# Conditioning columns from small fp32 products in a transformer layer

## The chip, the cores and the metric

The kernel runs on one core of a Trainium2 chip. The metric is the time of one execution on the device, in microseconds. The engines of the core are TensorE (PE, matrix products; PEld is its loading of the stationary operand), VectorE (DVE), ScalarE (ACT), GpSimd (POOL) and SyncE (SP), whose queue issues most DMA transfers.

## The reference, cut to what matters

One layer: two gated feed-forward networks with a token mixer between them (attention heads and mLSTM heads), on 256 tokens of width 2048, all in fp32. Each of the three parts is conditioned by a shift, a scale and a gate, nine vectors of 2048 that come from one row `c`:

```python
ada = (jax.nn.silu(c) @ w_ada + b_ada)[:, None, :]
sh1, sc1, g1, sh2, sc2, g2, sh3, sc3, g3 = jnp.split(ada, N_ADA, axis=-1)
h = _swiglu(_modulate(x, sh1, sc1), ffn1_w_in, ffn1_w_out)
x = _layernorm(ALPHA * x + 0.5 * (1 + g1) * h, ln1_g, ln1_b)
h = _token_mixer(_modulate(x, sh2, sc2), ...)
...
```

`_modulate(x, shift, scale)` is `_layernorm(x) * (1 + scale) + shift`. `w_ada` has 2048 rows of 18432 columns, 151 MB.

## The kernel before, in words

The feed-forward networks and the mixer run on TensorE. Weights arrive as fp32, ACT rounds them to fp32r (`hi`, L142), DVE forms the rest (`lo`, L143), and three products (L369 to L371) replace one of fp32. The tokens are columns (256 moving columns) in most stages and rows (512 moving columns) in the output projections. The stages in the profile's names: `s` and `gu_f` the input side of the first network, `o_f` its output projection, `mo`, `pr_f`, `pr_m`, `b_fv` the mixer's inputs, `o_mx` its output projection, `ge`, `fh`, `gf`, `fs` and `gu_f` the second network.

The nine conditioning vectors are summed beside this work. For 1024 columns at a time, 16 row tiles `ar` of 128 x 1024 are loaded (512 KB each, two buffers), and DVE multiplies each with its column of silu(c) and adds it to `acc` (L155, L157), so that `acc` holds 128 partial sums per column, one in each partition. What is left is the sum over the partitions.

- `first_ada0` and `first_ada` make shift and scale of the first part at the start; `first_columns` (L716) sums with eight products per 1024 columns that have `acc` as stationary operand and a column of ones as moving operand.
- `ada_pair(v, js)` makes shift and scale of the other two parts, v = 3 and v = 6. A set, one `j`, is 512 columns of the shift and the same 512 of the scale. The result is wanted as columns, features over the partitions, in `scsh`. For each half `i`, `ada_split` splits 512 columns into `ahi` (ACT) and `alo` (DVE); two pauses later `ada_sum` (L170) sums with two products that have the ones as stationary operand. That leaves the sums as a row, the same in each partition, in `bc`; a multiplication with the identity (`dg`, L188) and a reduction (L190) pick each feature's own partition, and a last add brings in the bias (L192).
- `ada_gate` makes the three gates, which are wanted as rows, with the same `ada_split` and `ada_sum`.

The sets and gates form one queue of generators, `ada_queue`. The big stages call `pump(n)` at fixed places: it takes `n` steps of the queue, a step being one row tile, and stops for this call at a pause (`PAUSE`); what it was owed stays owed. `need(n)` empties the queue up to the n-th part before a place that needs it, without regard to pauses. `pinned` puts what a step issues on an engine behind the newest split of weights on that engine. The order on each engine is otherwise made by a list scheduler from the order in the program and from buffers that come free. At the two boundaries between the parts the order of DVE and ACT is written out by hand.

The small buffers of the pool `ap` are shared by tag: `ahi` and `alo` of 2 KB per partition, `acc` of 4 KB, `araw` twice 4 KB. `tri`, `crow` and `brow` are used at the start only, in the places of the tags `ahi` and `alo`.

Of the kernel before, what the change touches and what calls it, by code (L numbers as in the profile page):

```python
# [7 lines left out]
F32 = mybir.dt.float32  # L8
F32R = mybir.dt.float32r
AF = mybir.ActivationFunctionType  # L10
ALU = mybir.AluOpType
AX = mybir.AxisListType
PSUM = bass.MemoryType.PSUM

P = 128
T = 256
D = 2048
KD = D // P
# [14 lines left out]
def layer_kernel(  # L33
# [8 lines left out]
    V, S, G_, PE, SP = nc.vector, nc.scalar, nc.gpsimd, nc.tensor, nc.sync  # L42
# [16 lines left out]
    ap = ctx.enter_context(tc.tile_pool(name="ap", bufs=1))  # L59
# [7 lines left out]
    def aux_tile(name):  # L67
        return pa.tile([P, 512], F32, tag="aux", name=name)


    ident = cst.tile([P, P], F32, name="ident")
    G_.memset(ident, 0.0)
    G_.affine_select(out=ident, in_=ident, compare_op=ALU.not_equal, fill=1.0, base=0,
                     pattern=[[-1, P]], channel_multiplier=1)
    tri = ap.tile([P, 2 * P], F32, tag="ahi", name="tri")
    G_.memset(tri, 1.0)
    G_.affine_select(out=tri[:, :P], in_=tri[:, :P], compare_op=ALU.is_ge, fill=0.0, base=0,
                     pattern=[[1, P]], channel_multiplier=-1)
# [3 lines left out]
    ones, onesr = triu1[:, P:], trir[:, P:]  # L82


    crow = ap.tile([KD, P], F32, tag="alo", name="crow")
    SP.dma_start(crow, c[0].rearrange("(k p) -> k p", p=P))
    res = cst.tile([P, 2, D], F32, name="res")
    for a in range(2):
# [7 lines left out]
    bcol = cst.tile([P, 9, KD], F32, name="bcol")  # L96
# [2 lines left out]
    G_.memset(mhalf, -0.5)  # L99

    def load_bcol():
        brow = ap.tile([72, 2, P], F32, tag="ahi", name="brow")
        SP.dma_start(brow, b_ada[0].rearrange("(h r p) -> r h p", h=2, p=P))
        bps = aux_tile("bps")
        for i in range(2):
            PE.transpose(bps[:, i * 72:(i + 1) * 72], brow[:, i, :], ident[:72, :72])
        V.tensor_copy(bcol.rearrange("p v k -> p (v k)"), bps[:, :144])
        for v in (1, 4, 7):
            V.tensor_scalar_add(bcol[:, v, :], bcol[:, v, :], 1.0)
# [31 lines left out]
    def split(src, hi, lo):  # L141
        S.copy(hi, src)  # L142
        return V.tensor_tensor(out=lo, in0=src, in1=hi.bitcast(F32), op=ALU.subtract)  # L143


    scsh = cst.tile([P, 9, KD], F32, name="scsh")
# [3 lines left out]
    def pair_cols(v, j):  # L150
        return w_ada[0, :, v * D:(v + 2) * D].rearrange("k (v n) -> k v n", v=2)[:, :, j * 512:(j + 1) * 512]

    def ada_acc(acc, raw, k):
        if k == 0:
            V.tensor_scalar_mul(acc, raw, csil[:, k:k + 1])  # L155
        else:
            V.scalar_tensor_tensor(out=acc, in0=raw, scalar=csil[:, k:k + 1], in1=acc,  # L157
                                   op0=ALU.mult, op1=ALU.add)


    def ada_split(acc, tag):
        ahi = ap.tile([P, 512], F32R, tag="ahi", name=f"ahi{tag}")
        alo = ap.tile([P, 512], F32R, tag="alo", name=f"alo{tag}")
        split(acc, ahi, alo)
        return ahi, alo

    def ada_sum(parts, tag):
        bc = aux_tile(f"bc{tag}")
        for i in range(2):
            PE.matmul(bc, onesr, parts[i], start=i == 0, stop=i == 1)  # L170
        return bc

    def ada_pair(v, js):
        for j in js:
            src = pair_cols(v, j)
            acc = ap.tile([P, 2, 512], F32, tag="acc", name=f"acc{v}_{j}")
            for k in range(KD):
                raw = ap.tile([P, 2, 512], F32, tag="araw", bufs=2, name=f"ar{v}_{j}_{k}")
                SP.dma_start(raw, src[k * P:(k + 1) * P])
                ada_acc(acc, raw, k)  # L180
                yield
            for i in range(2):
                parts = ada_split(acc[:, i, :], f"{v}_{j}_{i}")
                for _ in range(2):
                    yield PAUSE
                bc = ada_sum(parts, f"{v}_{j}_{i}")
                dg = ap.tile([P, 4, P], F32, tag="alo", name=f"dg{v}_{j}_{i}")
                V.tensor_tensor(out=dg, in0=bc.rearrange("p (a b) -> p a b", b=P),  # L188
                                in1=ident.unsqueeze(1).to_broadcast([P, 4, P]), op=ALU.mult)
                V.tensor_reduce(out=scsh[:, v + i, j * 4:(j + 1) * 4], in_=dg, axis=AX.X, op=ALU.add)  # L190
            cs = scsh[:, v:v + 2, j * 4:(j + 1) * 4]
            V.tensor_tensor(out=cs, in0=cs, in1=bcol[:, v:v + 2, j * 4:(j + 1) * 4], op=ALU.add)  # L192

    def ada_gate(v, s):
        for j in range(2):
            c0 = v * D + j * 1024
            acc = ap.tile([P, 1024], F32, tag="acc", name=f"acc{v}_{j}")
            for k in range(KD):
                raw = ap.tile([P, 1024], F32, tag="araw", bufs=2, name=f"ar{v}_{j}_{k}")
                SP.dma_start(raw, w_ada[0, k * P:(k + 1) * P, c0:c0 + 1024])  # L200
                ada_acc(acc, raw, k)
                yield
            for i in range(2):
                parts = ada_split(acc[:, i * 512:(i + 1) * 512], f"{v}_{j}_{i}")
                yield PAUSE
                if i == 0:
                    G_.dma_start(gate[:, j * 1024:(j + 1) * 1024], b_ada[0:1, c0:c0 + 1024].to_broadcast([P, 1024]))
                yield PAUSE
                bc = ada_sum(parts, f"{v}_{j}_{i}")
                gs = gate[:, j * 1024 + i * 512:j * 1024 + (i + 1) * 512]  # L210
                V.scalar_tensor_tensor(out=gs, in0=bc, scalar=1.0, in1=gs, op0=ALU.add, op1=ALU.add)
                if s != 1.0:
                    V.tensor_scalar_mul(gs, gs, s)

    ada_left = {}
    PAUSE = 1
# [450 lines left out]
    def entry_of(load, got, u0, u1):  # L667
        for u in range(u0, u1):
            got[u] = []
            for item in load(u):  # L670
                got[u].append(item)
                yield
# [181 lines left out]
    for k in range(KD):  # L854
        next(fa)
        if k == 4:
            load_bcol()
    with tc.manual_schedule(engines={mybir.EngineType.DVE, mybir.EngineType.Activation}):
        next(fa)
    ada_queue(ada_gate(2, 0.5), ada_pair(3, range(4)), ada_pair(6, range(2)), ada_gate(5, 1.0),  # L860
              ada_pair(6, range(2, 3)), ada_pair(6, range(3, 4)), ada_gate(8, 0.5))
    for j in range(4):
        fa = first_ada(j + 1) if j < 3 else load_mixer_smalls()
# [73 lines left out]
    fence, _, xs, ws = boundary(*ent["f"], lgb, 3, "1", xT, entry_of(mo_load, mow, 3, 6), KD, raws)  # L937
# [459 lines left out]
    for j in range(2, 10):  # L1397
# [6 lines left out]
        for f in range(2):  # L1404
            i = 2 * j + f
# [10 lines left out]
    for j in range(2, 10):  # L1416
# [7 lines left out]
        for f in range(2):  # L1424
            i = 2 * j + f
# [51 lines left out]
```

## Time and profile before

| | |
|---|---|
| times of 3 runs | 1929.67, 1932.37, 1935.84 us; median 1932.37 |
| profiled execution | 1936.38 us, of which span 1934.7 us |
| mean granted clock of TensorE | 0.994 |
| DMA | 510.90 MB, mean 264 GB/s |
| row tiles issued from SP in `w_ada` | 227 of 512 KB, 5.6 us from issue to landing |
| first and last sum of a pair (L188) | 500.3 and 1308.9 us |

The columns of a row of groups are: line, engine, operation, output and inputs by the program's names, shapes and count, then the busy time and the mean of one in ns, then the idle time of the engine just before them and what ended it. A row of the timeline has start and length in us; `x4` merges four records, and an idle time before it stands in brackets with what ended it.

### The profile page before, as it was taken

To read this page: it belongs to the slowest core of one execution; us is meant where nothing else is said; L and a number is where in the kernel's file an instruction comes from. 1 tells how busy PE (TensorE), PEld (TensorE's weight loads), DVE (VectorE), ACT (ScalarE), POOL (GpSimd) and SP (SyncE) were. 2 spreads that over 40 slices of the span, in tenths; PEclk is the share of its full clock that TensorE was granted. 3 is DMA by queue.
4 is the path that set the end of the run, shared out by engine and by line. 5 is a ranking of instruction groups with operands and counts; after the bars stand their busy time and mean duration, and the time that the engine had idled before them with its cause. 6 is when DMAs were issued, how large, how long until landed. Compare 5 with 4: busy or idle time off the path is not lost.

```text
span 1934.7 us, 32285 instructions
## 1 busy us (share of the span) xinstructions
PE 1895.6 (98%) x13085; PEld 1722.5 (89%) x13085; DVE 1485.6 (77%) x1838; ACT 954.6 (49%) x1352; POOL 56.3 (3%) x82
## 2 busy tenths in 40 slices
PE   6999999999999999999999999999999999999997
PEld 3999999999988888698998786999999999988886
DVE  5779989777889898888888789777766665555776
ACT  3554454443454555845755545555444444444552
POOL 1111100000000000100000000000000000000000
PEclk8999999999999999999999999999999999999999
DMA  9978969899998786498888884997776776655552
GB/s 352 372 260 317 324 222 318 296 309 312 304 337 311 264 302 222 155 325 297 274 293 285 278 289 173 300 307 247 253 252 227 261 238 196 238 185 188 194 196 87
DMA packets 295709, 510.90 MB, mean 264 GB/s; under 512 B 10850, under 2 KB 158722, under 8 KB 294536
## 3 DMA queue, kind: packets, MB, share of 16 engines
q1 hardware_dynamic: 287784, 480.53, 73.3%
q0 software_dynamic: 7776, 28.32, 4.2%
q8 instruction: 102, 1.67, 0.3%
q14 instruction: 47, 0.39, 0.1%
HBM read 506.71 MB, written 2.10 MB: 263 GB/s over the span
## 4 chain that ended last, share of the span: by engine, by line
PE 78%; issue 11%; DMA 6%; DVE 3%; ACT 1%; POOL 0%; SPq 0%; DVEq 0%; ACTq 0%; POOLq 0%
PE gu_f L369 8%; PE gu_f L371 8%; PE gu_f L370 8%; PE o_f L369 8%; PE o_f L371 8%; PE o_f L370 8%; PE s L369 4%; PE s L371 4%; PE s L370 4%; DMA ar<-in_w_ada_dram 3%; PE fh L369 2%; PE fh L371 2%; PE fh L370 2%; PE fs L369 1%; PE fs L370 1%
## 5 line engine op out<-in xcount | busy, mean ns | idle before, releaser
L157 DVE SCALAR_TENSOR_TENSOR acc<-ar,csil,acc 128x1024 f32<-128x1024 f32 x242 | 308.0, 1274 | 84.4 <-DMA ar<-in_w_ada_dram 82.8
L369 PE MATMUL s<-xhi_f,hi_s 128*128 128x256 f32 x768 | 213.2, 278 | 1.1 <-ACT hT1a L825 1.1
L370 PE MATMUL s<-xlo_f,hi_s 128*128 128x256 f32 x768 | 213.1, 277 | 0.0
L371 PE MATMUL s<-xhi_f,lo_s 128*128 128x256 f32 x768 | 212.8, 277 | 0.0
L371 PE MATMUL gu_f<-xhi_f,lo_f2i 128*128 128x256 f32 x768 | 212.0, 276 | 0.0
L369 PE MATMUL gu_f<-xhi_f,hi_f2i 128*128 128x256 f32 x768 | 212.0, 276 | 0.0
L370 PE MATMUL gu_f<-xlo_f,hi_f2i 128*128 128x256 f32 x768 | 212.0, 276 | 0.0
L143 DVE TENSOR_TENSOR lo_f2i<-raw_f2i,hi_f2i 128x1024 fp32r<-128x1024 f32 x96 | 117.5, 1224 | 88.3 <-ACT hi_f2i L142 88.2
L371 PE MATMUL gu_f<-xhi_f,lo_f1i 128*128 128x256 f32 x640 | 176.7, 276 | 0.0
L369 PE MATMUL gu_f<-xhi_f,hi_f1i 128*128 128x256 f32 x640 | 176.7, 276 | 0.0
L370 PE MATMUL gu_f<-xlo_f,hi_f1i 128*128 128x256 f32 x640 | 176.7, 276 | 0.0
L142 ACT CAST hi_f2i<-raw_f2i 128x1024 fp32r<-128x1024 f32 x96 | 100.8, 1050 | 135.1 <-PE gu_f L370 124.3
L142 ACT CAST hi_s<-raw_s 128x1024 fp32r<-128x1024 f32 x96 | 100.3, 1052 | 130.1 <-PE s L370 83.7
L369 PEld LDWEIGHTS s<-xhi_f,hi_s 128*128 128x128 f32 x768 | 144.7, 189 | 1.3 <-ACT hT1a L825 1.3
L370 PEld LDWEIGHTS s<-xlo_f,hi_s 128*128 128x128 f32 x768 | 144.9, 189 | 0.2 <-DVE xlo_f L300 0.2
L371 PEld LDWEIGHTS s<-xhi_f,lo_s 128*128 128x128 f32 x768 | 144.9, 189 | 0.0
L370 PEld LDWEIGHTS gu_f<-xlo_f,hi_f2i 128*128 128x128 f32 x768 | 144.1, 188 | 0.2
L369 PEld LDWEIGHTS gu_f<-xhi_f,hi_f2i 128*128 128x128 f32 x768 | 144.1, 188 | 0.2
L371 PEld LDWEIGHTS gu_f<-xhi_f,lo_f2i 128*128 128x128 f32 x768 | 144.1, 188 | 0.0
L143 DVE TENSOR_TENSOR lo_f2o<-raw_f2o,hi_f2o 128x1024 fp32r<-128x1024 f32 x88 | 107.8, 1225 | 44.9 <-ACT hi_f2o L142 44.8
L143 DVE TENSOR_TENSOR lo_s<-raw_s,hi_s 128x1024 fp32r<-128x1024 f32 x96 | 115.8, 1223 | 29.0 <-ACT hi_s L142 29.0
L369 PE MATMUL o_f<-hi_f2o,hh 128*128 128x512 f32 x344 | 135.2, 393 | 0.0
(502 smaller groups left out, 5383.9 us busy)
## 6 DMA issues: line engine op xcount, KB each, us to landing
ar<-in_w_ada_dram SPq DMA_DIRECT2D x227, 512.0 KB, 5.6
raw_f2i<-in_ffn_w_in_dram SPq DMA_DIRECT2D x48, 1024.0 KB, 5.2
raw_s<-in_ffn_w_in_dram SPq DMA_DIRECT2D x47, 1024.0 KB, 7.4
raw_f1o<-in_ffn_w_out_dram SPq DMA_DIRECT2D x44, 1024.0 KB, 6.7
raw_f2o<-in_ffn_w_out_dram SPq DMA_DIRECT2D x44, 1024.0 KB, 5.0
raw_f1i<-in_ffn_w_in_dram SPq DMA_DIRECT2D x40, 1024.0 KB, 7.8
ar<-in_w_ada_dram POOLq DMA_DIRECT2D x48, 512.0 KB, 6.9
raw_mxo<-in_w_out_dram SPq DMA_DIRECT2D x16, 1024.0 KB, 6.3
```

The lines of the kernel that those rows point to most:

```text
L142: S.copy(hi, src)
L143: return V.tensor_tensor(out=lo, in0=src, in1=hi.bitcast(F32), op=ALU.subtract)
L157: V.scalar_tensor_tensor(out=acc, in0=raw, scalar=csil[:, k:k + 1], in1=acc, op0=ALU.mult, op1=ALU.add)
L369: PE.matmul(o, ah, bh, start=start, stop=False)
L370: PE.matmul(o, ah, bl, start=False, stop=False)
L371: PE.matmul(o, al, bh, start=False, stop=stop)
```

## The change

A set of `ada_pair` is no longer split. ACT copies the 1024 sums of `acc` as they are into `rows`; four pauses in a row follow, where there were two in each half; then eight fp32 products, each with 128 columns of `rows` as stationary operand and one column of ones as moving operand, put the sums into `cp` (a PSUM tile `cc`) as columns, and one DVE add brings in the bias and writes `scsh`. The two tags `ahi` and `alo` become one tag `as` of 4 KB, which `ada_split` of the gates uses as one tile with two parts; `tri` and `brow` move to `as`, `crow` to `acc`.

```diff
-    tri = ap.tile([P, 2 * P], F32, tag="ahi", name="tri")
+    tri = ap.tile([P, 2 * P], F32, tag="as", name="tri")
...
-    crow = ap.tile([KD, P], F32, tag="alo", name="crow")
+    crow = ap.tile([KD, P], F32, tag="acc", name="crow")
...
-        brow = ap.tile([72, 2, P], F32, tag="ahi", name="brow")
+        brow = ap.tile([72, 2, P], F32, tag="as", name="brow")
...
     def ada_split(acc, tag):
-        ahi = ap.tile([P, 512], F32R, tag="ahi", name=f"ahi{tag}")
-        alo = ap.tile([P, 512], F32R, tag="alo", name=f"alo{tag}")
-        split(acc, ahi, alo)
-        return ahi, alo
+        parts = ap.tile([P, 2, 512], F32R, tag="as", name=f"as{tag}")
+        split(acc, parts[:, 0, :], parts[:, 1, :])
+        return parts[:, 0, :], parts[:, 1, :]
...
                 yield
+            rows = ap.tile([P, 2, 512], F32, tag="as", name=f"rows{v}_{j}")
+            S.copy(rows, acc)
+            for _ in range(4):
+                yield PAUSE
+            cp = aux_tile(f"cc{v}_{j}")[:, :8].rearrange("p (v k) -> p v k", v=2)
             for i in range(2):
-                parts = ada_split(acc[:, i, :], f"{v}_{j}_{i}")
-                for _ in range(2):
-                    yield PAUSE
-                bc = ada_sum(parts, f"{v}_{j}_{i}")
-                dg = ap.tile([P, 4, P], F32, tag="alo", name=f"dg{v}_{j}_{i}")
-                V.tensor_tensor(out=dg, in0=bc.rearrange("p (a b) -> p a b", b=P),
-                                in1=ident.unsqueeze(1).to_broadcast([P, 4, P]), op=ALU.mult)
-                V.tensor_reduce(out=scsh[:, v + i, j * 4:(j + 1) * 4], in_=dg, axis=AX.X, op=ALU.add)
-            cs = scsh[:, v:v + 2, j * 4:(j + 1) * 4]
-            V.tensor_tensor(out=cs, in0=cs, in1=bcol[:, v:v + 2, j * 4:(j + 1) * 4], op=ALU.add)
+                for q in range(4):
+                    PE.matmul(cp[:, i, q:q + 1], rows[:, i, q * P:(q + 1) * P], ones[:, 0:1], start=True, stop=True)
+            V.tensor_tensor(out=scsh[:, v:v + 2, j * 4:(j + 1) * 4], in0=cp, in1=bcol[:, v:v + 2, j * 4:(j + 1) * 4],
+                            op=ALU.add)
```

## The prediction

> **What bounds the kernel now.** I read the page first, for the engines and for the chain that ended last.
>
> ```profile
> span 1934.7 us, 32285 instructions
> PE 1895.6 (98%) x13085; PEld 1722.5 (89%) x13085; DVE 1485.6 (77%) x1838; ACT 954.6 (49%) x1352; POOL 56.3 (3%) x82
> PE 78%; issue 11%; DMA 6%; DVE 3%; ACT 1%; POOL 0%; SPq 0%; DVEq 0%; ACTq 0%; POOLq 0%
> ```
>
> TensorE (PE) is busy for 98% of the span, VectorE (DVE) for 77%, and the chain runs through PE for 78%. Matmuls are pipelined, so a busy PE need not be a full one. The second view is therefore the table of stretches, to see where PE really stands still.
>
> ```profile
> 40.00:1640.00 1600.00, 1587.93 (x11611) 1476.05 (x11610) 1274.02 (x1589) 808.90 (x1174) 48.16 (x66) 1.00 0.82 277
> 820.00:1005.00 185.00, 183.09 (x1376) 174.32 (x1376) 156.38 (x245) 105.53 (x185) 0.00 (x0) 0.99 0.90 302
> 1005.00:1165.00 160.00, 154.08 (x898) 133.53 (x897) 126.33 (x166) 79.16 (x139) 2.24 (x2) 1.00 0.84 281
> 1165.00:1215.00 50.00, 48.10 (x179) 31.44 (x179) 44.19 (x89) 30.06 (x58) 4.72 (x5) 1.00 0.52 179
> ```
>
> The columns after the length are the busy times of PE, PEld (its weight loads), DVE, ACT and POOL, then clock, DMA share and GB/s. Between 40 and 1640 us PE is idle for 1600.00 - 1587.93 = 12.07 us. Of these 1.91 lie in 820 to 1005 us, 5.92 in 1005 to 1165 us and 1.90 in 1165 to 1215 us: the token mixer and the boundary behind it hold 9.7 of the 12.07. Elsewhere PE has its next operand every time. All eight sets of columns that the change touches are made inside this stretch, as the rows below show. The third view is the list of PE's waits in the same stretch.
>
> ```profile
> PE ptp L1093 <- ACT s L1088: 2.5, 2, 1.4
> PE sps L1201 <- DVE dm L1207: 1.9, 1, 1.9
> PE ptp L1093 <- DVE gate L211: 1.6, 1, 1.6
> PE o_mx L370 <- DVE lo_mxo L143: 1.2, 2, 0.7
> PE s L369 <- ACT hT1a L825: 1.1, 1, 1.1
> ```
>
> No wait of PE is put down to `dg`, `scsh` or a row transfer of a pair. What the change takes off DVE is nowhere the thing that PE waits for last, by these rows; what it puts on PE has no idle time to fall into.
>
> **The change part by part: PE.** One set is 2 x 512 columns (`ada_pair`, one `j`). Before, each half costs two matmuls of `onesr` with 512 moving columns. The timeline of one half:
>
> ```profile
> 499.21 0.28 PE L371 MATMUL gu_f<-xhi_f,lo_f1i 128*128 128x256 f32 x1
> 499.55 0.28 PE L371 MATMUL gu_f<-xhi_f,lo_f1i 128*128 128x256 f32 x1
> 499.68 0.39 PE L170 MATMUL bc<-ahi,trir 128*128 128x512 f32 x1
> 499.91 0.39 PE L170 MATMUL bc<-alo,trir 128*128 128x512 f32 x1
> 500.14 0.28 PE L369 MATMUL gu_f<-xhi_f,hi_f1i 128*128 128x256 f32 x1
> 500.26 0.28 PE L370 MATMUL gu_f<-xlo_f,hi_f1i 128*128 128x256 f32 x1
> ```
>
> I count from start to start, since the durations (0.39) overlap. Three plain matmuls take 499.55 - 499.21 = 0.34 us, so 0.113 each. From 499.55 to 500.26 are 0.71 us and hold two plain ones (0.23), so the two `bc` matmuls cost 0.48 us. A set has two halves: 0.96 us.
>
> After, a set is eight fp32 products of 128 stationary columns with one moving column. The trace has this very form: `first_columns` (L716) does it for the first pair.
>
> ```profile
> 241.53 0.28 PE L371 MATMUL s<-xhi_f,lo_s 128*128 128x256 f32 x1
> 241.64 0.28 PE L369 MATMUL s<-xhi_f,hi_s 128*128 128x256 f32 x1
> 241.76 0.50 PE L716 MATMUL cp<-trir,acc 128*128 128x1 f32 x4
> 242.12 0.58 PE L716 MATMUL cq<-trir,acc 128*128 128x1 f32 x4
> 242.56 0.36 PE L370 MATMUL s<-xlo_f,hi_s 128*128 128x256 f32 x1
> 242.76 0.28 PE L371 MATMUL s<-xhi_f,lo_s 128*128 128x256 f32 x1
> ```
>
> These are two calls of `column`, two products each; four products leave eight records, so an fp32 product is two records. From 241.53 to 242.76 are 1.23 us and hold three plain matmuls (0.34): eight records take 0.89 us, 0.11 each, as long as a plain matmul of 256 columns. The sixteen records of a set cost 1.78 us. PE so pays 1.78 - 0.96 = 0.82 us more per set. There are two pairs of four sets each: 8 x 0.82 = **+6.6 us on PE**.
>
> **DVE and ACT.** The groups that shrink or go:
>
> ```profile
> L143 DVE TENSOR_TENSOR alo<-acc,ahi 128x512 fp32r<-128x512 f32 x28 | 19.2, 687 | 0.6 <-DVE scsh L190 0.5
> L188 DVE TENSOR_TENSOR dg<-bc,ident 128x512 f32<-128x512 f32 x16 | 11.0, 688 | 3.4 <-PE bc L170 3.2
> L190 DVE TENSOR_REDUCE scsh<-dg 128x4 f32<-128x512 f32 x16 | 10.9, 681 | 0.2
> L142 ACT CAST ahi<-acc 128x512 fp32r<-128x512 f32 x28 | 17.4, 623 | 24.8 <-DVE acc L157 24.4
> L142 ACT CAST hi_f1i<-raw_f1i 128x1024 fp32r<-128x1024 f32 x80 | 83.2, 1049 | 100.1 <-PE gu_f L370 68.1 <-DMA raw_f1i<-in_ffn_w_in_dram 23.0 <-PE s L370 3.6
> L192 DVE TENSOR_TENSOR scsh<-scsh,bcol x8: 159/164/167, 516.0 to 1311.4; 128x8 f32<-128x8 f32 x8
> L192 DVE TENSOR_TENSOR scsh<-scsh,bcol x2: 159/163/167, 901.6 to 976.5; 128x8 f32<-128x8 f32 x2
> ```
>
> Sixteen `dg` are the sixteen halves; the other twelve of the 28 `alo` belong to the gates and stay. DVE loses 16 x (0.687 + 0.688 + 0.681) = 32.9 us. Its last add stays (eight in all, two of them between 820 and 1005 us), of 128x8 with one operand now in PSUM; I leave it at 0.16. ACT gives up 16 x 0.62 = 10.0 us and gains eight copies of 1024 columns, about 1.05 each by the nearest row (`hi_f1i`), 8.4 in all.
>
> I book nothing of the 32.9 us. The `hi_f1i` row says why: ACT stood still 68.1 us until PE freed a `hi` buffer, so splits of weights are ahead of PE, and a DVE that is done sooner waits longer for the same buffers. In the mixer the largest wait that names DVE, `sps` behind `dm` (1.9 us), does not shrink either: its chain passes a table load of ACT, which the change leaves.
>
> ```profile
> 946.73 1.28 ACT L1205 ACT_TABLE_LOAD   x1
> 1163.50 0.62 ACT L142 CAST ahi<-acc 128x512 fp32r<-128x512 f32 x1 [2.42 <-DVE acc L157]
> 1165.63 2.00 ACT L142 CAST hi_mxo<-raw_mxo 128x1024 fp32r<-128x1024 f32 x2 [1.51 <-DMA raw_mxo<-in_w_out_dram]
> ```
>
> The longer copy adds a wait of 0.43 us for what is queued behind it on ACT. The tightest place is the end of the mixer's output projection, where `hi_mxo` comes next and idles 1.51 us for its transfer: the 0.43 is covered. Without that cover it would cost 0.43 us once.
>
> **Queue, buffers, start.** A set still gives sixteen row steps and four pauses, so the products sit where the second half's sum sat, and the row steps behind them keep their places. `acc` comes free after one copy and no longer after the second half's split; that can only let the next set's rows be loaded sooner. A set takes one `aux` slot of PSUM once where it took one twice. Renaming the buffers moves `crow`, `tri` and `brow`.
>
> ```profile
> L92 PE MATMUL cps<-ident,crow x1: 253/253/253, 2.6 to 2.6; 16*128 16x16 f32 x1
> L759 ACT COPY shifts<-row x1: 575/575/575, 34.2 to 34.2; 1x512 f32<-1x512 f32 x1
> ```
>
> `crow` is read at 2.6 us; `shifts`, which follows it in the buffer `acc`, is written at 34.2, so nothing waits. `tri` and `brow` follow each other in one buffer as before. These edits I price at zero; if one did wait it would be in the first 40 us, and the cover is 30 us wide.
>
> **The sum.** The profiled execution took 1936.38 us, 1.7 around its span, and 4.0 more than the median of the three times (1932.37). On it: 1936.4 + 6.6 = 1943.0. On the median: 1932.4 + 6.6 = **1939.0 us**. A difference of 0.3% (5.8 us) is about what a measurement of this kernel can tell from no change.
>
> **Rivals.** *First, on the other side: the freed VectorE time takes back PE's idle time.* Place: the mixer and its boundary, 820 to 1215 us, where DVE is busy 79 to 88% and PE's waits sit. Two sets (8.2 us of DVE, a quarter of the 32.9) end there at 901.6 and 976.5 us, in front of most of those waits, and `acc` free sooner lets the rows of the following gate start sooner. At most all 12.07 us go: 6.6 - 12.07 = -5.5, so 1926.9 us. It beats the cost once more than 6.6 of the 12.07 vanish; with the mixer's 9.7 alone it gives 1929.3. For it: the waits on `gate` and `lo_mxo` end with DVE work. Against it: together they are 2.8 us, and the largest hang on ACT. Chance 0.25; the three times before differ by 6 us, so part of it (0.09) would read as faster by over 0.3%, the rest (0.16) as no change.
>
> *Second: the stationary loads hide, and a one-column product costs next to nothing.* Then a set costs PE less than before. Against it stand the 0.11 us per record above. If a record cost nothing the sum would be -8 x 0.96 = -7.7, if half of 0.11, -0.6; I take the middle, 1928.2 us. Chance 0.03, within 0.3%. [...]
>
> *Third: the rows run ahead and push the weights back.*
>
> ```profile
> SPq L179 <- DVE acc L157: 139.0, 101, 3.1
> ar<-in_w_ada_dram SPq DMA_DIRECT2D x227, 512.0 KB, 5.6
> ```
>
> The queue of SP issues rows and weights in one order and stood 139.0 us on `acc` updates. If rows of the next set are put ahead of weights, one late landing (5.6 us) can reach PE. Two of them, for the two sets in 820 to 1005 us with its DMA share of 0.90, give 6.6 + 11.2 = 17.8: 1950.2 us. Against it: weights are ahead of PE, and PE's waits name no weight transfer. Chance 0.12.
>
> **How the numbers follow.** Forecast 0.60 (0.48 over 5.8 us, 0.12 below it, its own range 1937.0 to 1941.4, a quarter to a third of 6.6 either way for scheduling around the blocks), rivals 0.25, 0.03, 0.12. Slower: 0.48 + 0.12 = 0.60. Within 0.3%: 0.12 + 0.16 + 0.03 = 0.31. Faster: 0.09. The range runs from 1926.9 (all idle time gone) to 1932.4 + 6.6 + 5.6 = 1944.6 (one late landing) and leaves out the faster tail and half of the third rival.
>
> **What would show it.** The eight sets should appear as blocks of sixteen `cc` records, 1.7 to 1.9 us from neighbour to neighbour; DVE should be busy near 1453 us, ACT near 953; PE's idle time from 40 to 1640 us should stay at 11 to 13 us and the span grow by PE's 6.6. A block at 1 us or less, or idle time that falls by more than 3 us, refutes the forecast; PE waiting for casts behind weight transfers would show the third rival.

## The result, and the profile after

The changed kernel takes 1940.01 us (median of ten runs, 1936.55 to 1948.55), the kernel before in the same session 1933.68 us (1929.67 to 1938.69). The ratio is 1.0031, 95% interval 1.0018 to 1.0044: slower by 6.0 us (3.5 to 8.5). The forecast was +6.6 us.

The head of the page after, the groups of ACT's copy and of the last add, and the stretch of 40 to 1640 us (PE, PEld, DVE, ACT, POOL busy, clock, DMA share, GB/s):

```profile
span 1946.8 us, 32432 instructions
PE 1903.1 (98%) x13181; PEld 1734.1 (89%) x13181; DVE 1457.0 (75%) x1790; ACT 952.4 (49%) x1344; POOL 56.4 (3%) x82
...
L182 ACT COPY rows<-acc 128x1024 f32<-128x1024 f32 x8 | 8.4, 1054 | 10.7 <-DVE acc L157 10.5
...
L189 DVE TENSOR_TENSOR scsh<-cc,bcol x8: 156/160/169, 526.6 to 1318.2; 128x8 f32<-128x8 f32 x8
...
40.00:1640.00 1600.00, 1585.61 (x11597) 1476.80 (x11596) 1237.10 (x1529) 801.00 (x1158) 48.17 (x66) 1.00 0.82 275
```

DVE lost 28.6 us of work and ACT 2.2, and PE gained 7.5: work went from VectorE to TensorE as planned. A block of products in the timeline (start, length, engine and line; `x16` merges sixteen records; the lines are two lower than before):

```profile
517.13 0.28 PE L368 MATMUL gu_f<-xlo_f,hi_f1i 128*128 128x256 f32 x1
517.24 0.28 PE L369 MATMUL gu_f<-xhi_f,lo_f1i 128*128 128x256 f32 x1
517.36 1.84 PE L188 MATMUL cc<-trir,rows 128*128 128x1 f32 x16
519.06 0.36 PE L367 MATMUL gu_f<-xhi_f,hi_f1i 128*128 128x256 f32 x1
519.26 0.28 PE L368 MATMUL gu_f<-xlo_f,hi_f1i 128*128 128x256 f32 x1
```

From 517.24 to 519.26 are 2.02 us, less two plain matmuls (0.23): 1.79 us for a set.

**This profile is 12.1 us longer than the one before, and half of that is not the change.** Compared instruction by instruction, PE, DVE, ACT and POOL do the same work in the same order in both kernels for the first 330 us, and yet the last matmul of stage `s` starts 6.5 us later (312.6 and 319.1 us). The next fence has that row of the kernel before and of this profile, then the two places where PE waited for row sums of the first pair, and the stretch behind each:

```profile
L371 PE MATMUL s<-xhi_f,lo_s x768: 276/276/420, 39.7 to 312.6; 128*128 128x256 f32 x192
```

```profile
L369 PE MATMUL s<-xhi_f,lo_s x768: 276/276/419, 36.8 to 319.1; 128*128 128x256 f32 x192
...
171.38 0.61 PE L714 MATMUL cp<-trir,gate 128*128 128x1 f32 x4 [1.07 <-DVE gate L157]
244.19 0.60 PE L714 MATMUL cp<-trir,acc 128*128 128x1 f32 x4 [1.27 <-DVE acc L157]
...
173.60:180.60 7.00, 7.00 (x35) 7.00 (x35) 3.65 (x8) 3.04 (x8) 0.57 (x1) 0.51 0.97 334
245.30:248.80 3.50, 3.50 (x19) 3.50 (x18) 2.05 (x6) 1.62 (x4) 0.00 (x0) 0.51 0.57 219
```

PE waited 1.07 and 1.27 us for row sums that came late in this execution, and shortly after these waits the granted clock was 0.51 for 7.0 and 3.5 us. This is chance of the execution and no work of the renamed buffers: the eight other profiles below whose kernels start in the same way end the stage at 309.8 to 312.3 us. This run, 1948.55 us, is also the slowest of its ten. A second profile of the same kernel (run e5 below) has a quiet start, so its stages can be set against the kernel before. The number after "to" is the start of the last matmul of a stage. First the kernel before:

```profile
L371 PE MATMUL s<-xhi_f,lo_s x768: 276/276/420, 39.7 to 312.6; 128*128 128x256 f32 x192
L371 PE MATMUL gu_f<-xhi_f,lo_f1i x640: 276/276/285, 313.0 to 533.2; 128*128 128x256 f32 x160
L371 PE MATMUL o_f<-hi_f1o,hl x336: 388/391/396, 539.3 to 778.1; 128*128 128x512 f32 x168
L371 PE MATMUL fh<-xhi_f,lo_fh x256: 276/276/285, 1216.2 to 1304.8; 128*128 128x256 f32 x128
L371 PE MATMUL gf<-hi_gu,xlo_f x32: 388/391/398, 1305.8 to 1330.5; 128*128 128x512 f32 x32
L371 PE MATMUL o_f<-hi_f2o,hl x344: 388/391/396, 1686.5 to 1922.0; 128*128 128x512 f32 x172
```

Then the changed kernel in its second profile, with its stretch of 40 to 1640 us:

```profile
L369 PE MATMUL s<-xhi_f,lo_s x768: 276/276/415, 37.7 to 310.1; 128*128 128x256 f32 x192
L369 PE MATMUL gu_f<-xhi_f,lo_f1i x640: 276/276/285, 310.4 to 531.4; 128*128 128x256 f32 x160
L369 PE MATMUL o_f<-hi_f1o,hl x336: 388/391/396, 537.6 to 778.6; 128*128 128x512 f32 x168
L369 PE MATMUL fh<-xhi_f,lo_fh x256: 276/276/283, 1219.1 to 1308.6; 128*128 128x256 f32 x128
L369 PE MATMUL gf<-hi_gu,xlo_f x32: 388/391/398, 1310.9 to 1335.0; 128*128 128x512 f32 x32
L369 PE MATMUL o_f<-hi_f2o,hl x344: 388/391/396, 1691.0 to 1926.5; 128*128 128x512 f32 x172
...
40.00:1640.00 1600.00, 1588.48 (x11663) 1478.73 (x11663) 1241.63 (x1532) 805.46 (x1160) 48.18 (x66) 1.00 0.81 276
```

Subtract neighbours. Stage `gu_f` of the first network: 220.6, then 221.3 us, +0.7 with one set in it. `o_f`: 244.9, then 247.2, +2.3 with three sets. From there to the end of `fh`, with mixer and boundaries: 526.7, then 530.0, +3.3 with three sets. `gf`: 25.7, then 26.4, +0.7 with one set. From `gf` to the end of `o_f`: 591.5 both times, with no set. The sum is +7.0 us for eight sets, 0.9 each. (The span grew by 4.5 us, since stage `s` ended 2.5 us earlier here than in the kernel before.) PE's idle time is 11.5 us in place of 12.07.

The five sets outside the mixer are the clean part: +3.7 us, 0.74 each. It is less than the 0.82 that was booked in part because in two of these five sets the old form's second half stood as two single products, which took about 0.6 us in place of 0.48. The mixer's +3.3 us is not the products alone. The same stretch lasts 526.4 us in the first profile of the changed kernel and 530.2 in run e3 below, whose products cost PE no more than before: the mixer moves by 3 to 4 us from one execution to the next.

### The profile page after: what moved, and what is told of

It reads as the page before. It is cut to its first block, busy times and chain, and to the rows that moved or that the text cites. A ratio compares the mean times of both kernels' runs of the same rounds, so it can differ in the third digit from the quotient of the medians.

```text
span 1946.8 us, 32432 instructions
## 1 busy us (share of the span) xinstructions
PE 1903.1 (98%) x13181; PEld 1734.1 (89%) x13181; DVE 1457.0 (75%) x1790; ACT 952.4 (49%) x1344; POOL 56.4 (3%) x82
## 4 chain that ended last, share of the span: by engine, by line
PE 77%; DMA 11%; DVE 5%; issue 4%; ACT 2%; POOL 1%; SPq 0%; DVEq 0%; POOLq 0%; ACTq 0%
PE o_f L367 8%; PE gu_f L367 8%; PE gu_f L369 8%; PE gu_f L368 8%; PE o_f L369 8%; PE o_f L368 8%; DMA ar<-in_w_ada_dram 7%; PE s L367 3%; PE s L369 3%; PE s L368 3%; DVE acc L157 2%; PE fh L367 2%; PE fh L369 1%; PE fh L368 1%; PE fs L368 1%
```

## The experiments

Theory P: TensorE pays about 0.11 us for every record of a product and the time freed on VectorE is worth nothing. Its rivals: the loads hide (H), VectorE's time comes back (D), rows that run ahead make the loss (R). Each run is set against runs of the kernel before on its chip; a time in us is the ratio less one, times 1934 us.

**e1_twice: each product twice.**

```diff
+                    for _ in range(2):
                         PE.matmul(cp[:, i, q:q + 1], rows[:, i, q * P:(q + 1) * P], ones[:, 0:1], start=True, stop=True)
```

> Each of the eight products of a set is issued twice, the second over the first. Theory P (TensorE pays 0.11 us for each of a set's records, and nothing hides them): 8 sets x 16 more records x 0.111 us = +14.2 us over the changed kernel, so about 20.5 us over the kernel before, ratio near 1.0106. Rival H (the loads of the stationary operand hide behind other work, the loss comes from elsewhere): no more than 2 us over the changed kernel. Rival D (freed VectorE time pays part back) says nothing else here than P.

Measured: 1.0166 (1.0147 to 1.0185), +32.1 us, 25.5 more than the changed kernel (6.6, the mean of its two ratios). H falls. But P's 14.2 is 11 us short, so something else came with the second sixteen records. The timeline behind a block, and stretches of 8 us behind blocks:

```profile
509.42 3.63 PE L189 MATMUL cc<-trir,rows 128*128 128x1 f32 x32
...
513.35 0.28 PE L368 MATMUL gu_f<-xhi_f,hi_f1i 128*128 128x256 f32 x1
513.46 0.33 PE L369 MATMUL gu_f<-xlo_f,hi_f1i 128*128 128x256 f32 x1
513.60 0.41 PE L370 MATMUL gu_f<-xhi_f,lo_f1i 128*128 128x256 f32 x1
513.81 0.41 PE L368 MATMUL gu_f<-xhi_f,hi_f1i 128*128 128x256 f32 x1
...
512.80:520.80 8.00, 8.00 (x58) 8.00 (x58) 5.17 (x7) 1.66 (x2) 0.00 (x0) 0.79 0.84 274
688.20:696.20 8.00, 8.00 (x24) 6.39 (x25) 6.64 (x8) 1.58 (x2) 0.00 (x0) 0.61 0.85 261
992.80:1000.80 8.00, 8.00 (x70) 7.95 (x70) 5.51 (x7) 3.55 (x8) 0.00 (x0) 1.00 0.95 309
...
40.00:1640.00 1600.00, 1593.78 (x11623) 1483.51 (x11623) 1234.16 (x1525) 798.63 (x1153) 48.16 (x66) 0.99 0.81 274
```

Behind the block the step from matmul to matmul goes from 0.11 to 0.21 us (513.60 to 513.81), and the mean clock of the next 8 us is 0.79. Six of the eight blocks have 0.79 behind them, one 0.61, one 1.00. At half clock 0.79 means 3.4 us, which lose 1.7 us of work; seven such blocks lose 6 x 1.7 + 3.1 = 13 us. The mixer took some back: PE's idle time from 40 to 1640 us is 6.2 us here (last row), some 5 us less than in the quiet profile of the changed kernel. Together 14.2 + 13 - 5 = 22 us, at the lower end of what the interval allows (21.8 to 29.2). The clock was found after the run, so it needed a test.

**e9_twice_apart, e10_twice_again: is it the length of the block?** The same doubled products, sixteen records at a time:

```diff
-            for _ in range(4):
-                yield PAUSE
+            for _ in range(2):
+                yield PAUSE
...
+            for turn in range(2):
+                if turn:
+                    for _ in range(2):
+                        yield PAUSE
                 for i in range(2):
```

> The doubled products of the run e1_twice, as two blocks of sixteen records with two pauses between them (two pauses stand before the first). In e1_twice the granted clock fell to half for 3.4 us behind seven of the eight blocks of 32 records. Theory G (a block of 3.6 us of one-column products trips the clock, one of 1.8 us does not): no half clock behind the blocks, and the price of the records alone, 14.2 us over the changed kernel, ratio 1.009 to 1.012. Rival S (e1_twice was slow for another reason, the longer hold of rows or the order of the queue): as slow as e1_twice, ratio 1.015 to 1.0185.

> The kernel of e1_twice once more beside the run above. Both theories: ratio 1.0147 to 1.0185, and the clock at half behind most of the blocks.

Measured on one chip: 1.0105 (1.0087 to 1.0122) apart, 1.0160 (1.0144 to 1.0176) in one block. The same records on PE, and 10.6 us between them. Apart, they cost 20.3 - 6.6 = 13.7 us, against 14.2 by P. The agreement to half a us is partly luck, since PE's idle time is 6.4 us here too; the table under e7 is the cleaner measure. From the profile of the kernel apart, three of its blocks, and the 8 us behind four:

```profile
496.83 1.84 PE L192 MATMUL cc<-trir,rows 128*128 128x1 f32 x16
760.13 3.63 PE L192 MATMUL cc<-trir,rows 128*128 128x1 f32 x32
1313.94 3.63 PE L192 MATMUL cc<-trir,rows 128*128 128x1 f32 x32
...
498.40:506.40 8.00, 8.00 (x72) 8.00 (x72) 5.63 (x5) 2.11 (x2) 0.00 (x0) 1.00 1.08 368
763.50:771.50 8.00, 8.00 (x37) 6.59 (x37) 1.90 (x3) 0.00 (x0) 0.00 (x0) 1.00 0.41 131
1247.50:1255.50 8.00, 8.00 (x72) 8.00 (x72) 6.35 (x7) 2.52 (x3) 0.00 (x0) 1.00 0.76 244
1317.30:1325.30 8.00, 8.00 (x30) 6.46 (x30) 2.67 (x5) 1.62 (x3) 0.00 (x0) 0.79 0.43 137
```

None of its twelve single blocks has a slower clock behind it (1.00 over the 8 us behind each). Where `need` skips the pauses, two blocks run together, at 760 and at 1314 us; behind the first the clock is 1.00, behind the second 0.79 again. In e10 the mean granted clock of the five runs is 0.986 to 0.988, in e9 0.992 to 0.994, and a block of e10 took 4.64 us in place of 3.63:

```profile
508.48 4.64 PE L189 MATMUL cc<-trir,rows 128*128 128x1 f32 x32
```

S falls: the same records and the same work on VectorE cost 10.6 us more in one block than in two.

**e7_fp32r: half the records.**

```diff
-            rows = ap.tile([P, 2, 512], F32, tag="as", ...)
+            rows = ap.tile([P, 2, 512], F32R, tag="as", ...)
...
-                    PE.matmul(cp[:, i, q:q + 1], ..., ones[:, 0:1], ...)
+                    PE.matmul(cp[:, i, q, :], ..., onesr[:, 0:2], ...)
```

> The changed kernel with rows rounded to fp32r by the copy and the products in fp32r with two moving columns of ones, the second result unused: one record per product instead of two, 64 in all instead of 128. The sums are sums of rounded numbers. Theory P: 64 x 0.111 = 7.1 us less than the changed kernel, so about 0.8 us less than the kernel before, ratio 0.9985 to 1.0005. Rival R (the loss of the changed kernel is rows that run ahead or the other order of the queue): as slow as the changed kernel, 1.002 to 1.0045.

Measured: 0.9996 (0.9984 to 1.0009), -0.8 us. Order of the queue, copy, pauses and VectorE are those of the changed kernel; half the records are gone, and with them its whole loss. R falls. A block now:

```profile
509.38 0.28 PE L369 MATMUL gu_f<-xhi_f,lo_f1i 128*128 128x256 f32 x1
509.49 0.95 PE L188 MATMUL cc<-trir,rows 128*128 128x2 f32 x8
510.30 0.36 PE L367 MATMUL gu_f<-xhi_f,hi_f1i 128*128 128x256 f32 x1
510.50 0.28 PE L368 MATMUL gu_f<-xlo_f,hi_f1i 128*128 128x256 f32 x1
```

From 509.38 to 510.50 are 1.12 us, less 0.23: 0.89, half of 1.79.

The two stages in which PE has next to no idle time show the price of a record most cleanly. Their lengths in us, by the starts of the last matmuls as above:

| stage | sets in it | before | changed (e5) | half the records (e7) | twice, apart (e9) |
|---|---|---|---|---|---|
| `gu_f` | 1 | 220.6 | 221.3 | 220.4 | 223.2 |
| `o_f` | 3 | 244.9 | 247.2 | 244.5 | 252.5 |

Against the changed kernel a set is 0.9 us shorter in e7, with 8 records fewer, and 1.8 to 1.9 us longer in e9, with 16 more: 0.11 to 0.12 us per record.

**e2_one_product: one product of eight moving columns in place of eight products; the sums of the other columns are left out.**

```diff
-            for i in range(2):
-                for q in range(4):
-                    PE.matmul(cp[:, i, q:q + 1], rows[:, i, q * P:(q + 1) * P], ones[:, 0:1], ...)
+            PE.matmul(cp, rows[:, 0, :P], ones[:, 0:8].rearrange("p (v k) -> p v k", v=2), ...)
```

> One product with eight moving columns takes the place of a set's eight, so the other seven blocks of 128 columns are left out and scsh is not what it should be. VectorE and ScalarE do what they do in the changed kernel. Theory P: two records (0.22 us) in place of the 0.96 us before, so 8 x 0.74 = 5.9 us less than the kernel before, ratio 0.997; the freed 33 us of VectorE add nothing. Rival D: on top of that up to 12 us of TensorE's idle time go, ratio 0.991 to 0.995. Rival R (the loss of the changed kernel comes from rows that run ahead, not from products): about as slow as the changed kernel, 1.002 to 1.003.

Measured: 0.9980 (0.9966 to 0.9994), -3.9 us; P's -5.9 lies inside the interval, D's 0.991 to 0.995 outside.

**e3_light_dve and e4_dve_back: what VectorE's time is worth.** The first has the PE work of before and the light VectorE; it leaves out `alo` and the picking by the identity, so its columns are not the sums. The second has the PE work of after and the VectorE work of before:

```diff
-                parts = ada_split(acc[:, i, :], ...)
+                ahi = ap.tile([P, 512], F32R, tag="ahi", ...)
+                S.copy(ahi, acc[:, i, :])
...
-                V.tensor_tensor(out=dg, in0=bc..., in1=ident..., op=ALU.mult)
-                V.tensor_reduce(out=scsh[:, v + i, j * 4:(j + 1) * 4], in_=dg, ...)
+                bcs.append(ada_sum((ahi, ahi), ...))
```

```diff
             S.copy(rows, acc)
+            for i in range(2):
+                V.tensor_tensor(out=acc[:, i, :], in0=acc[:, i, :], in1=rows[:, i, :], op=ALU.subtract)
...
+            for i in range(2):
+                V.tensor_tensor(out=r, in0=r, in1=ident..., op=ALU.mult)
+                V.tensor_reduce(out=rows[:, i, 0:4], in_=r, axis=AX.X, op=ALU.add)
```

> The kernel before with its four products of 512 columns per set, but the rounded half twice as operand (alo is left out), and the multiplication with the identity and the reduction left out too; an add of four columns stands for them, so scsh is not what it should be. TensorE has the work of before, VectorE about 33 us less. Theory P: within 2 us of the kernel before, ratio 0.999 to 1.001. Rival D: faster, by up to 12 us, ratio down to 0.994.

> The changed kernel with the VectorE work of before put back on top, on tiles that nobody reads any more: two subtractions of 512 columns after the copy, two multiplications with the identity and two reductions after the products (about 33 us in all). The result is that of the changed kernel. Theory P: the time of the changed kernel within 2 us, about 6.3 us over the kernel before, ratio 1.002 to 1.0045. Rival D (the change got part of its cost back from VectorE): clearly slower than the changed kernel, ratio 1.006 or more.

Measured: 1.0011 (0.9998 to 1.0024) for the first, 1.0046 (1.0028 to 1.0063) for the second. The stretch of 40 to 1640 us of the first:

```profile
40.00:1640.00 1600.00, 1586.39 (x11578) 1474.74 (x11579) 1244.81 (x1544) 807.21 (x1171) 48.16 (x66) 1.00 0.82 277
```

DVE is 29.2 us lighter than before (1274.02), PE's idle time is 13.6 us instead of 12.07, and the time is not better by more than 0.4 us at the interval's end. Thirty us of VectorE bought nothing. The second run is less sharp: its 1.0046 lies just above the 1.0045 that P allowed, and against the changed kernel (1.0031 and 1.0037) it is slower by 2 us on the mean, inside the spread. Its stages narrow this down. `gu_f`, `o_f` and `gf` take 221.3, 247.2 and 26.4 us, to a tenth what they take in e5, so VectorE's work costs nothing there; in the mixer's stretch it takes 531.3 us against 530.0, less than that stretch moves by itself.

**e5_after_again and e8_pause0: the pauses.**

```diff
-            for _ in range(4):
-                yield PAUSE
```

> The changed kernel once more, on the chip and beside the runs of the three kernels that follow, so that they can be compared with it. All theories: 1.002 to 1.0045 of the kernel before, as on record.

> The changed kernel with no pause between the copy and the products of a set. Theory P: the products cost TensorE the same; the copy must now be done when TensorE gets there, so between the changed kernel's time and 8 x 1.05 us (one copy) more: ratio 1.003 to 1.008. Rival Q (the queue, which gets 32 steps ahead, ends the gate of the mixer sooner and takes TensorE's waits there): faster than the changed kernel by 2 to 6 us, ratio 1.000 to 1.002.

Measured: 1.0037 (1.0021 to 1.0052) for the changed kernel, 1.0040 (1.0026 to 1.0054) without pauses. The two are the same; Q falls, and so does the upper end of P's range, eight exposed copies (1.008): with no pause the copy still costs PE little, and none of PE's waits in that profile is for `rows`.

**e6_hi_only: fewer products in the old form.** The other way that P points to: the old form costs 0.48 us per half for two products, so give up one.

```diff
-        for i in range(2):
-            PE.matmul(bc, onesr, parts[i], start=i == 0, stop=i == 1)
+        PE.matmul(bc, onesr, parts, start=True, stop=True)
```

> The kernel before, but the sums over the partitions take the rounded half alone, one product of 512 columns instead of two, in the pairs and in the gates; alo and its subtraction are left out, so the conditioning vectors are sums of rounded numbers. Theory P: 28 products of 0.24 us less on TensorE, 6.7 us less than the kernel before, ratio 0.9965 (0.995 to 0.998). Rival H (products of this kind hide behind other work): no change, 0.999 to 1.001.

Measured: 0.9970 (0.9955 to 0.9984), -5.8 us. Of the versions that form all the sums it is the one that beats both kernels; its price is the low half of the conditioning sums, not time.

## Why the prediction was right

- **PE's price.** 0.82 us per set was booked, from start to start in `first_columns`; a block takes 1.79 us in place of 1.78. Half the records (e7) and twice the records, mostly in blocks of the same length (e9), moved the time by -7.4 and +13.7 us, where 0.111 us per record gives -7.1 and +14.2, and the stages without idle time give 0.11 to 0.12 us per record. This is shown.
- **VectorE at nothing.** DVE fell by 28.6 us on the page, where 32.9 were worked out and 1453 us of busy time were forecast (1457.0 came). The prediction counted PE from start to start but added up durations for DVE, and these overlap too: in the kernel before a `dg` that lasts 0.69 us starts at 500.34 and the next operation at 500.95, 0.61 us later; 48 records at 0.08 to 0.09 us are the difference. Since DVE was booked at nothing, it did not touch the sum. e3 shows that such a relief alone is worth 0.4 us at most. The reason given, splits that are ahead of PE and wait for buffers, was only argued; the measured zero stands without it.
- **The first rival** had a chance of 0.25. PE's idle time between 40 and 1640 us did not shrink by more than the 3 us that were allowed: 12.07 before, 14.4 and 11.5 in two profiles after; in its place, 820 to 1215 us, 9.7 before, 8.4 and 10.3 after. The 14.4 is outside the 11 to 13 that were foretold: 2.5 of it lie before 330 us, in the late start, and 1.6 are one wait at 544.8 us that the second profile does not have. "Elsewhere PE has its next operand every time" was a little too strong: 2.3 of the 12.07 us lie outside the mixer and its boundary.
- **The second rival**, loads that hide, falls with e1 and e7: more records cost more and fewer cost less, at 0.11 us each.
- **The third rival** would have shown as PE waiting for casts behind weight transfers. A small relative of it is there. In the second profile PE waited 1.41 us in the mixer for a split, `lo_m1b`, which had its turn on DVE behind two row updates, and these waited 0.85 and 0.30 us for their rows (fence below). The first profile has 0.9 us of this wait, the kernel before none. e7 has 1.6 us of it and is not slow, so the loss is not made of it; the rival had priced 11.2 us.
- **The copy** took 1054 ns (1.05 was taken), the last add 160 ns (0.16). ACT's page time fell by 2.2 us, where 10.0 - 8.4 = 1.6 were worked out.
- **Where it was lucky.** The span was to grow by 6.6 us; it grew by 12.1 in the first profile and by 4.5 in the second, so the sign that the prediction named came in neither. Only the stages show that 6.5 us of the first came before the first instruction that differs. That the ten runs agree with 6.6 so closely is also luck: the five sets outside the mixer cost 0.74 us each and not 0.82, and the mixer moves by half of the forecast. The median of ten runs was needed to see 6 us at all.

```profile
936.79 1.28 DVE L157 SCALAR_TENSOR_TENSOR acc<-ar,csil,acc 128x1024 f32<-128x1024 f32 x1 [0.85 <-DMA ar<-in_w_ada_dram]
938.77 1.29 DVE L157 SCALAR_TENSOR_TENSOR acc<-ar,csil,acc 128x1024 f32<-128x1024 f32 x1 [0.30 <-DMA ar<-in_w_ada_dram]
940.37 1.22 DVE L143 TENSOR_TENSOR lo_m1b<-raw_m1b,hi_m1b 128x1024 fp32r<-128x1024 f32 x1
941.64 0.38 PE L369 MATMUL pr_m<-xhi_mx,lo_m1b 128*128 128x256 f32 x1 [1.41 <-DVE lo_m1b L143]
```

## What to carry to other kernels

Where the matrix engine has no idle time, cost a replacement by the distance from one start to the next in a place where the profile already has the operation, and count records, not operations: a one-column fp32 product cost 0.22 us here (two records), as much as two matmuls of 256 columns (0.23). Count the other engines from start to start as well, since durations overlapped here too (0.69 us for `dg`, 0.61 to the next start). Thirty us taken off an engine that was 77% busy bought nothing here: PE's waits that ended with that engine's work came to 6.2 us between 40 and 1640 us before, and to 8.5 us in e3. And before a longer profile is explained, set its stages against those of the old one up to the first changed instruction.

## What the runs showed of the hardware

The granted clock fell to half although the engine was never idle: in e1 PE was busy for all of the 8 us behind each block, and the mean clock there was 0.79 behind six blocks and 0.61 behind one. So blocks of 32 records of one-column products (3.63 us in e1, with a load of the stationary operand for each record, 256 loads for 256 records) had 3.4 us or more of half clock behind them in seven of eight cases in e1; in e9 one of two had it (0.79). In e10, the kernel of e1 again, the mean granted clock was 0.987 in the profiled run, where that of e9 had 0.994.

Not every long block brought it: the clock was 1.00 from 992.8 to 1000.8 us in e1 and from 763.5 to 771.5 us in e9, each behind such a block. What set these two apart was not shown.

Blocks of 16 records (1.84 us) brought it in none of twelve cases in e9. In the changed kernel, with eight such blocks in each profile, the mean clock was 1.00 from 260 to 1640 us in the first profile and from 40 to 1640 us in the second; the price of a block there is its records, 1.79 us. Together with a wait even fewer products were followed by half clock: in the first profile 1.27 us of wait and 0.9 us of one-column products, at 244 us, and then a clock of 0.50 from 245.33 to 248.74 us, with PE busy all the while. Behind the wait of 1.07 us at 171 us it was 0.50 from 173.65 to 180.48 us.
